# RG-LRU gates of a hybrid encoder layer: two 64-channel blocks on the two row halves of the array

## The chip, the cores and the metric

The kernel runs on one core of one Trainium2 chip. The metric is the device time of one execution in microseconds, the median of several runs. One execution was also taken by the hardware profiler, and all rows shown here come from that one.

## The reference

A layer of 1024 tokens and 1024 channels. The input is normalised and projected, and the columns of the projection are split into query, key, value, the recurrence's input `u`, a GeLU branch `y` and two output gates `g`. Attention and a recurrent branch run on these, are gated and merged, and a feed-forward layer follows. What matters here is the recurrent branch: a depthwise convolution of width 4 over the tokens, and for each of two directions two gates that are block-diagonal products, sixteen blocks of 64 channels.

```python
def block_diag_linear(u, w, b):
    ub = u.reshape(bsz, s, N_REC_BLOCKS, REC_BLOCK)           # 16 blocks of 64
    return jnp.einsum('bsnc,ncd->bsnd', ub, w).reshape(bsz, s, c) + b

def rg_lru(u, w_a, b_a, w_i, b_i, lam, reverse):
    r_gate = sigmoid(block_diag_linear(u, w_a, b_a))
    i_gate = sigmoid(block_diag_linear(u, w_i, b_i))
    log_a = -LRU_C * r_gate * softplus(-lam)
    a = exp(log_a)
    bx = sqrt(max(-expm1(2 * log_a), 0)) * (i_gate * u)
    # h[t] = a[t] * h[t-1] + bx[t], forward or backward over the tokens
```

Both directions' `h` are added, multiplied by `gelu(y)`, and projected.

## The kernel before

**How work is kept.** All tiles have 128 partitions. Activations are held transposed: channels on partitions, 1024 tokens along the free dimension, so the 1024 channels of `u` are eight chunks `j` of 128 channels, and a chunk holds two blocks of 64. Products are made at the accuracy of float32 by splitting each operand into a high and a low part (`split`, line 398: a copy on ScalarE, a subtraction on VectorE) and adding three products: high by high, high by low, low by high. In the profile `wh`, `wl` are the parts of weights, `uh`, `ul` those of a chunk of `u` after the convolution.

**What sets the order.** The kernel doesn't issue instructions as it is written. Every call is recorded as an operation with a position (`SD(pos, fn)`, `M(fn)`), and `solve` (line 210) then runs a list scheduler: each engine takes the available operation with the lowest position, with a cost from a table (`op.cost`, line 179 for TensorE). Buffers are counted too: pool `t` has 45 tiles of SBUF, `w` 9, and PSUM has two banks `pm`, two `pr`, four `pa`. The result is a fixed order per engine; `issue` (line 332) writes it out, all from line 338, which is why every row of the profile names that line. A position is one entry of `main`, which in the projections is six matmuls.

**The stretch of the change.** `pairs` (line 644) makes the projections of `u`, `y`, `g`, `q`, `k` by a scheme with seven products for eight; they use banks `pm` and `pa`. Meanwhile the recurrence runs chunk by chunk (the loop `for j in range(8)`, line 877). Two chunks belong to one entry `("u", i)` of `PORD`; the second begins RSTEP positions after the first (line 848), and its steps stand at fixed positions after its base, divided by RRATE. The steps are:

- `uev`: ScalarE adds the projection's bias to `u`.
- `conv`: one scaled copy on ScalarE, three multiply-adds on VectorE, into `uc`.
- `ucs`: splits `uc` into `uh`, `ul`.
- `gate_pe` (line 909): for each gate (`ty`: 0 recurrence gate, 1 input gate) and direction `d`, six matmuls of 128x128 weights by 128x512 tokens into the two `pr` banks, one bank for each half of the tokens. The weights of a chunk are a 128x128 matrix with its two 64x64 blocks on the diagonal and zeros elsewhere.
- `gate_act` (line 921): a sigmoid on ScalarE from each bank, 512 columns at a time, with a bias per partition; this gives the bank back.
- `iu`, `tanh`, `exp`, `sq`, `m2`, `sqrt`, `scan`: the rest of the recurrence on ScalarE and VectorE; then both directions are added, multiplied by the loaded `y`, and stored as `recd`.

The weights of two chunks come by one load of 512 KB and two splits into pool `w` (`wgj`, line 880). After the projections come attention (from about 500 us, in between with the product of the recurrence's output, `tprod`, line 855) and the rest. `rec_split` (line 1133) splits the reloaded `recd` into `rh`, `rl` for that product. In attention, `a_av` (line 1086) multiplies probabilities `ab` by values `V`: two heads of 64 columns, written to the lower and upper half of the partitions of one bank. DMAs are all issued from SP, in order.

Of the kernel before, what the change touches and what calls it, by code (L numbers as in the profile page):

```python
# [24 lines left out]
for _name, _w in (("g1", 8), ("g2", 8), ("bq", 4), ("bk", 4), ("bu", 8), ("by", 8),  # L25
                  ("bga", 8), ("bgr", 8), ("cw", 32), ("cb", 8), ("ba", 16), ("bi", 16), ("lam", 16)):
    PC[_name] = _n
    _n += _w
# [78 lines left out]
class Plan:  # L107
# [11 lines left out]
    def add(self, eng, meth, args, kw):  # L119
# [57 lines left out]
        if eng == "pe":  # L177
            f32 = isinstance(args[1], VA) and args[1].base.dt == F32
            op.cost = n * 0.84 + 2.6 if meth == "transpose" else (12 if wr[0].box[0][0] else n * 1.68 + 40) if f32 else n * 0.417 + 13.3
# [170 lines left out]
def emit(tc, x, prm, wst, wv, wg, watt, wrec, wout, wff1, wff2, tb, bv, lnf, out):  # L350
# [6 lines left out]
    with ExitStack() as ctx:  # L357
# [490 lines left out]
        RSTEP, RRATE, AOFF, ASTEP = 33.0, 1.0, -6.0, 0.75  # L848
# [25 lines left out]
        wgj = [None] * 4  # L874
        SD(end_of["u", 0] - 12, softplus)

        for j in range(8):
            base = end_of["u", j // 2] + 0.3 + (j % 2) * RSTEP
            if j % 2 == 0:
                wgj[j // 2] = wjob(wg[j // 2], (P, 2, 4, P), base + 2, (22.0, 6.3, 6.0))  # L880
# [5 lines left out]
            def uev(R=R, j=j):  # L886
                R.u = us[j]
                act.activation(R.u, R.u, AF.Identity, bias=col("bu", j), scale=1.0)

            def conv(R=R, j=j):  # L890
                R.uc = T("uc")
                u = R.u
                act.activation(R.uc, u, AF.Identity, bias=col("cb", j), scale=col("cw", 16 + j))
# [7 lines left out]

            def ucs(R=R):
                R.hi = T("uh", F32R)
                R.lo = T("ul", F32R)
                split(R.hi, R.lo, R.uc)
# [3 lines left out]
            def gate_pe(ty, d, R=R, j=j):  # L909
                w = wgj[j // 2]  # L910
                wh = w.hi[:, j % 2, ty * 2 + d, :]
                wl = w.lo[:, j % 2, ty * 2 + d, :]
                pss = R.g[ty, d] = [PR(), PR()]
                for b in range(2):
                    pe.matmul(pss[b], wh, R.hi[:, b * 512:(b + 1) * 512], start=True, stop=False)
                for b in range(2):
                    pe.matmul(pss[b], wh, R.lo[:, b * 512:(b + 1) * 512], start=False, stop=False)
                for b in range(2):
                    pe.matmul(pss[b], wl, R.hi[:, b * 512:(b + 1) * 512], start=False, stop=True)

            def gate_act(ty, d, R=R, j=j):
                pss = R.g[ty, d]
                g = R.g[ty, d] = T("g")
                for b in range(2):
                    act.activation(g[:, b * 512:(b + 1) * 512], pss[b], AF.Sigmoid,
                                   bias=col("ba" if ty == 0 else "bi", d * 8 + j), scale=1.0)
# [40 lines left out]
            SD(base, uev, 30.0)  # L967
            at(1.0, conv)
            at(5.0, ucs)
            for gi, (ty, d) in enumerate(((0, 0), (1, 0), (0, 1), (1, 1))):  # L970
                at(7.5 + 2.5 * gi, lambda ty=ty, d=d, f=gate_pe: f(ty, d))
                at(9.3 + 2.5 * gi, lambda ty=ty, d=d, f=gate_act: f(ty, d))
# [584 lines left out]

def pack(inp):
# [3 lines left out]
    def vec(v):  # L1562
        return np.asarray(v).reshape(-1, P).T

    b_in = inp["b_in"][0]
    cols = [vec(inp["ln1_g"][0]), vec(inp["ln2_g"][0]), vec(b_in[0:512]), vec(b_in[512:1024]),
            vec(b_in[1536:2560]), vec(b_in[2560:3584]), vec(b_in[3584:4608]), vec(b_in[4608:5632]),
            vec(inp["conv_w"][0]), vec(inp["conv_b"][0]), vec(inp["b_rg_a"][0]), vec(inp["b_rg_i"][0]),
# [9 lines left out]
    wg = np.zeros((4, P, 2, 4, P), np.float32)  # L1578
    for ty, nme in enumerate(("w_rg_a", "w_rg_i")):
        w = inp[nme][0]  # L1580
        for d in range(2):
            for j in range(8):
                for b in range(2):
                    wg[j // 2, b * 64:(b + 1) * 64, j % 2, ty * 2 + d, b * 64:(b + 1) * 64] = w[d, 2 * j + b]
# [44 lines left out]
```

## Time and profile before

| | us |
|---|---|
| median of 3 runs | 1419.1 (1418.35 to 1420.6) |
| profiled execution | 1419.8 |
| its span, first to last instruction | 1418.0 |
| TensorE busy | 1402.9 (99%) |
| VectorE busy | 1041.9 (73%) |
| ScalarE busy | 852.0 (60%) |
| mean busy share of the DMA engines | 46% |

A matmul's record begins where it starts and ends when its last column has come out, so records of successive matmuls overlap: the spacing of starts tells what one costs, and a busy TensorE may hold pauses. Weight loads (PEld) are rows of their own, one ahead of each matmul. A row of a timeline can stand for several like instructions; its duration then runs from the first start to the last end.

### The profile page before, as it was taken

The page shows a single profiled execution, that of the slowest core. Times are in us where ns is not written, and L with a number is a line of the kernel's source. Part 1 is how long each engine was busy: PE and PEld are TensorE (multiplying, and loading weights), DVE is VectorE, ACT ScalarE, POOL GpSimd, SP SyncE. Part 2 cuts the span into 40 slices and gives each one's busy share as a digit, 9 for nine tenths or more (in the row PEclk, how much of TensorE's full clock was granted, in tenths as well). Part 3 has the DMA queues.
Part 4 walks back from the last instruction along what each step waited for, and adds up shares of the span by engine and source line. Part 5 has one row for each costly group of instructions (what it writes and reads, how often), then busy time and mean ns, then how long its engine had stood idle before and what let it go on. Part 6 is the DMA issues. An engine that isn't in the chain of part 4 may idle for free.

```text
span 1418.0 us, 17748 instructions
## 1 busy us (share of the span) xinstructions
PE 1402.9 (99%) x6568; PEld 1153.0 (81%) x6568; DVE 1041.9 (73%) x1595; ACT 852.0 (60%) x1316; POOL 0.7 (0%) x6
## 2 busy tenths in 40 slices
PE   8999999999999999999999999999999999999997
PEld 6878888888888887878888888888888888888886
DVE  6897788796985987763945777666666867848996
ACT  7758686877678776764535645654455634423544
POOL 0000000000000000000000000000000000000000
PEclk9999999999999999999999999999999999999999
DMA  6523224233233965747812236444448882245402
GB/s 218 161 62 134 104 97 155 75 134 137 86 104 119 345 225 202 255 146 265 328 61 103 100 116 223 175 156 145 163 163 295 310 327 98 76 173 183 149 15 104
DMA packets 87223, 230.09 MB, mean 162 GB/s; under 512 B 8544, under 2 KB 16864, under 8 KB 87136
## 3 DMA queue, kind: packets, MB, share of 16 engines
q1 hardware_dynamic: 87136, 228.96, 46.2%
q8 instruction: 51, 0.84, 0.2%
q14 instruction: 36, 0.29, 0.1%
HBM read 159.72 MB, written 69.21 MB: 161 GB/s over the span
## 4 chain that ended last, share of the span: by engine, by line
PE 98%; DVE 1%; ACT 0%; DMA 0%; issue 0%
PE pa L338 57%; PE pm L338 28%; PE pr L338 13%; DMA x<-in_x_dram 0%; DVE T4l L338 0%; DVE T1l L338 0%; ACT F L338 0%; DVE F L338 0%; ACT hTh L338 0%; ACT h L338 0%; DVE wl L338 0%; DVE sl L338 0%; DVE hTl L338 0%; DVE T3l L338 0%; DVE nu L338 0%
## 5 line engine op out<-in xcount | busy, mean ns | idle before, releaser
L338 PE MATMUL pa<-wh,rh 128*128 128x512 f32 x448 | 174.0, 389 | 0.0
L338 PE MATMUL pa<-wh,rl 128*128 128x512 f32 x448 | 174.0, 389 | 0.0
L338 PE MATMUL pa<-wl,rh 128*128 128x512 f32 x448 | 173.9, 389 | 0.0
L338 ACT ACTIVATE r<-r 128x1024 f32<-128x1024 f32 x64 | 67.5, 1059 | 67.9 <-DVE r L338 66.9
L338 DVE TENSOR_TENSOR sl<-ws,sh 128x1024 fp32r<-128x1024 f32 x72 | 87.0, 1219 | 19.1 <-ACT sh L338 18.9
L338 ACT ACTIVATE rh<-rs 128x1024 fp32r<-128x1024 f32 x56 | 58.6, 1049 | 67.6 <-PE pa L338 53.5
L338 DVE TENSOR_TENSOR wl<-ws,wh 128x1024 fp32r<-128x1024 f32 x64 | 77.6, 1218 | 29.1 <-ACT wh L338 27.9
L338 PEld LDWEIGHTS pa<-wl,rh 128*128 128x128 f32 x448 | 84.1, 188 | 17.6
L338 PEld LDWEIGHTS pa<-wh,rh 128*128 128x128 f32 x448 | 84.1, 188 | 17.5
L338 PEld LDWEIGHTS pa<-wh,rl 128*128 128x128 f32 x448 | 84.1, 188 | 17.3
L338 ACT ACTIVATE wh<-w 128x1024 fp32r<-128x1024 f32 x56 | 58.8, 1051 | 60.3 <-PE pa L338 44.1
L338 ACT ACTIVATE sh<-ws 128x1024 fp32r<-128x1024 f32 x72 | 75.3, 1054 | 28.0 <-DVE ws L338 27.3
L338 DVE TENSOR_TENSOR acc<-pa,acc 128x512 f32<-128x512 f32 x72 | 49.3, 687 | 51.2 <-PE pa L338 51.1
L338 DVE TENSOR_TENSOR r<-pa,r 128x512 f32<-128x512 f32 x74 | 50.9, 687 | 44.9 <-PE pa L338 44.3
L338 ACT ACTIVATE r<-pm 128x512 f32<-128x512 f32 x81 | 48.0, 592 | 52.5 <-PE pm L338 51.8
L338 ACT ACTIVATE wh<-ws 128x1024 fp32r<-128x1024 f32 x64 | 67.2, 1055 | 15.6 <-DMA ws<-in_watt_dram 8.4
L338 DVE TENSOR_TENSOR wl<-w,wh 128x1024 fp32r<-128x1024 f32 x56 | 68.1, 1218 | 9.3 <-ACT wh L338 5.9
L338 DVE TENSOR_TENSOR rl<-rs,rh 128x1024 fp32r<-128x1024 f32 x56 | 68.1, 1218 | 5.2 <-ACT rh L338 2.9
L338 PE MATMUL pm<-T4h,wx 128*128 128x512 f32 x216 | 71.4, 389 | 0.0
L338 PE MATMUL pa<-T1l,sh 128*128 128x512 f32 x144 | 56.2, 390 | 1.3 <-DVE T1l L338 1.3
L338 PE MATMUL pa<-T1h,sh 128*128 128x512 f32 x144 | 56.1, 389 | 0.0
L338 PE MATMUL pa<-T1h,sl 128*128 128x512 f32 x144 | 56.0, 389 | 0.0
(267 smaller groups left out, 3736.0 us busy)
## 6 DMA issues: line engine op xcount, KB each, us to landing
rs<-rd SPq DMA_DIRECT2D x56, 512.0 KB, 6.7
ws<-in_wst_dram SPq DMA_DIRECT2D x41, 512.0 KB, 4.1
ws<-in_wff_dram SPq DMA_DIRECT2D x38, 512.0 KB, 4.4
w<-in_wff_dram SPq DMA_DIRECT2D x32, 512.0 KB, 7.6
B<-in_tb_dram SPq DMA_DIRECT2D x32, 384.0 KB, 4.6
x<-in_x_dram SPq DMA_DIRECT2D x16, 512.0 KB, 7.8
gd<-r SPq DMA_DIRECT2D x16, 512.0 KB, 2.9
g<-gd SPq DMA_DIRECT2D x16, 512.0 KB, 7.1
```

The lines of the kernel that those rows point to most:

```text
L338: getattr(eng[op.eng], op.meth)(*[r(a) for a in op.args], **{k: r(a) for k, a in op.kw.items()})
```

## The change

The two blocks of a chunk are no longer two corners of one 128x128 matrix. Block 0's input channels lie on partitions 0 to 63, block 1's on 64 to 127, and each gets its own 64x128 weights: 64 columns for the recurrence gate and 64 for the input gate. A matmul then takes 64 partitions of `uh` or `ul`, and is built for a tile of 64 rows and 128 columns, at row 0 for block 0 and at row 64 for block 1. `gate_pe(d, b)` now runs over directions and halves of the tokens, and makes both gates of both blocks: three products for each block, written block 0, block 1, block 0, block 1 and so on, each block into a `pr` bank of its own. The number of matmuls (192) and their columns (512) stay.

Block 0's bank has the recurrence gate on the lower partitions and the input gate on the upper, block 1's the other way round. So after the sigmoids (as many as before, with their own bias columns) `gate_mv` makes three transfers of 64 partitions within SBUF for each direction: the two halves of the input gate into a new tile `gi`, and the missing half of the recurrence gate into block 0's tile, over the half that the first transfer has read.

Besides: the projection's bias of `u` goes into the convolution's constants (`conv_bias`), so `uev` goes, and two small subtractions per chunk mend the first two tokens and the last one, where the convolution sees padding. The weights of four chunks fit one load; they and their parts now live in pool `t`. The planner gets a cost for 64-row matmuls (263 ns of 512 columns for block 0, 12 ns for block 1), and RSTEP and RRATE are changed.

```diff
-            op.cost = n * 0.84 + 2.6 if meth == "transpose" else (12 if wr[0].box[0][0] else n * 1.68 + 40) if f32 else n * 0.417 + 13.3
+            rows = args[1].box[0] if isinstance(args[1], VA) else (0, P)
+            op.cost = (n * 0.417 + 50 if rows[0] == 0 else 12) if rows[1] - rows[0] == 64 else n * 0.84 + 2.6 if meth == "transpose" else (12 if wr[0].box[0][0] else n * 1.68 + 40) if f32 else n * 0.417 + 13.3
...
-        RSTEP, RRATE, AOFF, ASTEP = 33.0, 1.0, -6.0, 0.75
+        RSTEP, RRATE, AOFF, ASTEP = 28.0, 0.9, -6.0, 0.75
...
+        cvb, cve = C("cvb", [P, 8]), C("cve", [P, 8, 3])
+
+        def conv_bias():
+
+            t = C("cvt", [P, 4, 8])
+            for jj in range(4):
+                c = PC["cw"] + jj * 8
+                dve.tensor_mul(t[:, jj], pr[:, c:c + 8], pr[:, PC["bu"]:PC["bu"] + 8])
+            dve.tensor_add(cve[:, :, 0], t[:, 0], t[:, 1])
+            dve.tensor_copy(cve[:, :, 1], t[:, 0])
+            dve.tensor_copy(cve[:, :, 2], t[:, 3])
+            dve.tensor_add(cvb, t[:, 2], t[:, 3])
+            dve.tensor_add(cvb, cvb, cve[:, :, 0])
+            dve.tensor_add(cvb, cvb, pr[:, PC["cb"]:PC["cb"] + 8])
+
+        SD(end_of["u", 0] - 12, conv_bias)
...
-            if j % 2 == 0:
-                wgj[j // 2] = wjob(wg[j // 2], (P, 2, 4, P), base + 2, (22.0, 6.3, 6.0))
+            if j % 4 == 0:
+                wgj[j // 4] = wjob(wg[j // 4], (P, 4, 2, P), base + 2, (22.0, 6.3, 6.0), tag="t", stag="t")
...
-            def uev(R=R, j=j):
-                R.u = us[j]
-                act.activation(R.u, R.u, AF.Identity, bias=col("bu", j), scale=1.0)
+            def conv0(R=R, j=j):
+                R.uc = T("uc")
+                act.activation(R.uc, us[j], AF.Identity, bias=cvb[:, j:j + 1], scale=col("cw", 16 + j))
...
+                dve.tensor_sub(R.uc[:, 0:2], R.uc[:, 0:2], cve[:, j, 0:2])
+                dve.tensor_sub(R.uc[:, S - 1:S], R.uc[:, S - 1:S], cve[:, j, 2:3])
...
-            def gate_pe(ty, d, R=R, j=j):
-                w = wgj[j // 2]
-                wh = w.hi[:, j % 2, ty * 2 + d, :]
-                wl = w.lo[:, j % 2, ty * 2 + d, :]
-                pss = R.g[ty, d] = [PR(), PR()]
-                for b in range(2):
-                    pe.matmul(pss[b], wh, R.hi[:, b * 512:(b + 1) * 512], start=True, stop=False)
-                for b in range(2):
-                    pe.matmul(pss[b], wh, R.lo[:, b * 512:(b + 1) * 512], start=False, stop=False)
-                for b in range(2):
-                    pe.matmul(pss[b], wl, R.hi[:, b * 512:(b + 1) * 512], start=False, stop=True)
-
-            def gate_act(ty, d, R=R, j=j):
-                pss = R.g[ty, d]
-                g = R.g[ty, d] = T("g")
-                for b in range(2):
-                    act.activation(g[:, b * 512:(b + 1) * 512], pss[b], AF.Sigmoid,
-                                   bias=col("ba" if ty == 0 else "bi", d * 8 + j), scale=1.0)
+            def gate_pe(d, b, R=R, j=j):
+
+                w, c = wgj[j // 4], slice(b * 512, (b + 1) * 512)
+                pss = R.g["ps", d, b] = [PR(), PR()]
+                for wt, x in ((w.hi, R.hi), (w.hi, R.lo), (w.lo, R.hi)):
+                    for bl in range(2):
+                        r = slice(bl * 64, (bl + 1) * 64)
+                        pe.matmul(pss[bl], wt[r, j % 4, d, :], x[r, c], start=(wt is w.hi and x is R.hi),
+                                  stop=(wt is w.lo))
+
+            def gate_act(d, b, R=R, j=j):
+                for bl in range(2):
+                    if b == 0:
+                        R.g[bl, d] = T("g")
+                    act.activation(R.g[bl, d][:, b * 512:(b + 1) * 512], R.g["ps", d, b][bl],
+                                   AF.Sigmoid, bias=col("bg2", (d * 8 + j) * 2 + bl), scale=1.0)
+
+            def gate_mv(d, R=R):
+
+                g0, g1, gi = R.g[0, d], R.g[1, d], T("gi")
+                lo, hi = slice(0, 64), slice(64, P)
+                sp.dma_start(gi[lo], g0[hi])
+                sp.dma_start(gi[hi], g1[lo])
+                sp.dma_start(g0[hi], g1[hi])
+                R.g[1, d] = gi
...
-            SD(base, uev, 30.0)
+            SD(base, conv0, 30.0)
             at(1.0, conv)
             at(5.0, ucs)
-            for gi, (ty, d) in enumerate(((0, 0), (1, 0), (0, 1), (1, 1))):
-                at(7.5 + 2.5 * gi, lambda ty=ty, d=d, f=gate_pe: f(ty, d))
-                at(9.3 + 2.5 * gi, lambda ty=ty, d=d, f=gate_act: f(ty, d))
+            for gi, (d, b) in enumerate(((0, 0), (0, 1), (1, 0), (1, 1))):
+                at(7.5 + 2.5 * gi, lambda d=d, b=b, f=gate_pe: f(d, b))
+                at(9.3 + 2.5 * gi, lambda d=d, b=b, f=gate_act: f(d, b))
+                if b:
+                    at(9.4 + 2.5 * gi, lambda d=d, f=gate_mv: f(d))
...
-    wg = np.zeros((4, P, 2, 4, P), np.float32)
+
+    wg = np.empty((2, P, 4, 2, P), np.float32)
     for ty, nme in enumerate(("w_rg_a", "w_rg_i")):
         w = inp[nme][0]
         for d in range(2):
             for j in range(8):
                 for b in range(2):
-                    wg[j // 2, b * 64:(b + 1) * 64, j % 2, ty * 2 + d, b * 64:(b + 1) * 64] = w[d, 2 * j + b]
+                    wg[j // 4, b * 64:(b + 1) * 64, j % 4, d, (ty ^ b) * 64:((ty ^ b) + 1) * 64] = w[d, 2 * j + b]
```

TensorE's order in chunk 1 before: the second half of the input gate, forward, then the recurrence gate, backward. Names are out<-in; `pr_266`, `pr_270` and `pr_271` are banks of the gates, `pa_267` a product of the projections:

```order
L338 MATMUL pr_266_1630<-uh_255_1323,wh_182_1008 128x512
L338 MATMUL pr_266_1630<-ul_256_1485,wh_182_1008 128x512
L338 MATMUL pr_266_1630<-uh_255_1323,wl_183_1065 128x512
L338 MATMUL pa_267_1592<-T1h_158_908,sh_252_1526 128x512
L338 MATMUL pa_267_1592<-T1l_160_1023,sh_252_1526 128x512
L338 MATMUL pa_267_1592<-T1h_158_908,sl_253_1535 128x512
L338 MATMUL pr_270_1640<-uh_255_1323,wh_182_1008 128x512
L338 MATMUL pr_271_1645<-uh_255_1323,wh_182_1008 128x512
L338 MATMUL pr_270_1640<-ul_256_1485,wh_182_1008 128x512
L338 MATMUL pr_271_1645<-ul_256_1485,wh_182_1008 128x512
L338 MATMUL pr_270_1640<-uh_255_1323,wl_183_1065 128x512
L338 MATMUL pr_271_1645<-uh_255_1323,wl_183_1065 128x512
```

The same place after. `pr_267` is block 0's bank (rows 0 to 63), `pr_268` block 1's (rows 64 to 127), and likewise `pr_271` and `pr_272`:

```order
L339 MATMUL pr_267_1623<-uh_249_1523,wh_185_993 128x512
L339 MATMUL pr_267_1623<-ul_250_1579,wh_185_993 128x512
L339 MATMUL pr_267_1623<-uh_249_1523,wl_186_1078 128x512
L339 MATMUL pm_261_1514<-T2h_146_728,sh_251_1541 128x512
L339 MATMUL pm_261_1514<-T2l_148_892,sh_251_1541 128x512
L339 MATMUL pr_268_1634<-uh_249_1523,wh_185_993 128x512
L339 MATMUL pr_268_1634<-ul_250_1579,wh_185_993 128x512
L339 MATMUL pr_268_1634<-uh_249_1523,wl_186_1078 128x512
L339 MATMUL pm_261_1514<-T2h_146_728,sl_252_1556 128x512
```

Block 0's three matmuls stand together, two whole-array matmuls of the projection come between, and then block 1's three: written alternately, they are issued block by block. Further on the order has `pr_271` three times and `pr_272` three times right behind it.

SP's queue about chunk 4, before (`ws` are weight loads, `gd` and `recd` stores):

```order
L338 DMA recd_517_3242<-g_478_2935 128x1024
L338 DMA ws_539_3307<-in_wst_dram 128x1024
L338 DMA gd_544_3319<-r0_522_3197 128x1024
L338 DMA gd_543_3337<-r1_530_3252 128x1024
L338 DMA ws_549_3366<-in_wst_dram 128x1024
```

And after, with the six transfers of a chunk:

```order
L339 DMA gi_430_2635<-g_418_2593 64x1024
L339 DMA gi_430_2635<-g_419_2615 64x1024
L339 DMA recd_420_2667<-gi_375_2334 128x1024
L339 DMA g_418_2593<-g_419_2615 64x1024
L339 DMA gi_443_2686<-g_437_2656 64x1024
L339 DMA gi_443_2686<-g_438_2665 64x1024
L339 DMA g_437_2656<-g_438_2665 64x1024
L339 DMA ws_452_2760<-in_wst_dram 128x1024
```

The transfers stand ahead of a weight load, and the third of each set (`g_418<-g_419`, `g_437<-g_438`) writes what the first reads. SP's queue has 517 rows in place of 471.

## Rows read from the trace of the kernel before

**Rows 1.** The page: TensorE's busy time, and the chain that ended last, by engine.

```profile
PE 1402.9 (99%) x6568; PEld 1153.0 (81%) x6568; DVE 1041.9 (73%) x1595; ACT 852.0 (60%) x1316; POOL 0.7 (0%) x6
...
PE 98%; DVE 1%; ACT 0%; DMA 0%; issue 0%
```

**Rows 2.** Busy time by stretch, seven from 100 to 520 us; first and sum.

```profile
100.00:160.00 60.00, 60.00 (x266) 49.71 (x265) 45.79 (x53) 44.81 (x52) 0.00 (x0) 1.00 0.35 123
...
sum 420.00, PE 420.00 PEld 346.02 DVE 335.38 ACT 322.50 POOL 0.00; mean PE 60.00 PEld 49.43 DVE 47.91 ACT 46.07 POOL 0.00
```

**Rows 3.** Waits from 100 to 460 us: total, times, longest; TensorE's only row.

```profile
PEld pr L338 <- ACT g L338: 1.6, 6, 0.3
```

**Rows 4.** Timeline of TensorE, chunk 0's first gate: start, duration, instruction.

```profile
107.23 0.39 PE L338 MATMUL pm<-hTh,wh 128*128 128x512 f32 x1
...
107.91 0.62 PE L338 MATMUL pr<-uh,wh 128*128 128x512 f32 x2
108.36 0.39 PE L338 MATMUL pm<-hTh,wh 128*128 128x512 f32 x1
108.59 0.39 PE L338 MATMUL pm<-hTl,wh 128*128 128x512 f32 x1
```

**Rows 5.** Groups of TensorE: count, busy us, mean ns; one of three.

```profile
L338 PE MATMUL pr<-uh,wh 128*128 128x512 f32 x64 | 23.4, 398 | 0.0
```

**Rows 6.** Timeline of TensorE about a group of V products.

```profile
644.71 0.40 PE L338 MATMUL pr<-rh,wh 128*128 128x512 f32 x1
645.04 0.88 PE L338 MATMUL pa<-ab,V 128*64 128x128 f32 x12
645.84 0.50 PE L338 MATMUL pm<-rl,wh 128*128 128x512 f32 x1
646.18 0.40 PE L338 MATMUL pr<-rl,wh 128*128 128x512 f32 x1
```

**Rows 7.** Timeline of the weight loads about such a group, idle time before in brackets.

```profile
574.81 0.64 PEld L338 LDWEIGHTS pa<-ab,V 128*64 128x64 f32 x12 [0.35 <-issue]
575.61 0.19 PEld L338 LDWEIGHTS pr<-rl,wh 128*128 128x128 f32 x1 [0.17 <-issue]
```

**Rows 8.** Timeline of TensorE, a whole-array product and three transposes.

```profile
563.55 0.40 PE L338 MATMUL pr<-rh,wl 128*128 128x512 f32 x1
563.78 0.49 PE L338 MATMUL pa<-ident,ab 128*128 128x128 f32 x3
```

**Rows 9.** Groups of weight loads: 128 columns wide, and 64.

```profile
L338 PEld LDWEIGHTS pm<-rh,wh 128*128 128x128 f32 x64 | 12.0, 188 | 1.8
...
L338 PEld LDWEIGHTS pa<-ab,V 128*64 128x64 f32 x384 | 22.2, 136 | 11.0 <-issue 10.6 <-ACT ab L338 0.4
```

**Rows 10.** Groups of ScalarE and VectorE from 90 to 470 us.

```profile
L338 ACT ACTIVATE r<-r,pr 128x1024 f32<-128x1024 f32 x18 | 20.6, 1147 | 4.2 <-DVE r L338 4.2
L338 ACT ACTIVATE wh<-ws 128x1024 fp32r<-128x1024 f32 x21 | 22.1, 1052 | 0.4 <-PE pr L338 0.4
L338 DVE TENSOR_TENSOR sp<-sp,sp 128x16 f32<-128x16 f32 x9 | 1.5, 170 | 0.1
```

**Rows 11.** Transfers of 256 KB, us to landing; waits of SP and for weights.

```profile
V<-vd SPq DMA_DIRECT2D x16, 256.0 KB, 6.9
rd<-r SPq DMA_DIRECT2D x16, 256.0 KB, 2.2
SPq L338 <- PE pm L338: 66.2, 8, 16.8
ACT wx L338 <- DMA ws<-in_wst_dram: 0.7, 1, 0.7
```

**Rows 12.** Timelines: the last split of the recurrence's output, and TensorE's next product.

```profile
525.14 1.23 DVE L338 TENSOR_TENSOR rl<-rec,rh 128x1024 fp32r<-128x1024 f32 x1
527.34 0.40 PE L338 MATMUL pm<-rl,wh 128*128 128x512 f32 x1
```

More of the change, by code (lines that the diff above doesn't have):

```diff
@@ L25 @@
 for _name, _w in (("g1", 8), ("g2", 8), ("bq", 4), ("bk", 4), ("bu", 8), ("by", 8),
-                  ("bga", 8), ("bgr", 8), ("cw", 32), ("cb", 8), ("ba", 16), ("bi", 16), ("lam", 16)):
+                  ("bga", 8), ("bgr", 8), ("cw", 32), ("cb", 8), ("bg2", 32), ("lam", 16)):
     PC[_name] = _n
@@ L873, in emit @@
         rec, recd = [None] * 8, [None] * 8
[L874 removed]
+        wgj = [None] * 2
         SD(end_of["u", 0] - 12, softplus)
+        cvb, cve = C("cvb", [P, 8]), C("cve", [P, 8, 3])
[11 more added lines that the diff above has]
+        SD(end_of["u", 0] - 12, conv_bias)
         for j in range(8):
             base = end_of["u", j // 2] + 0.3 + (j % 2) * RSTEP
[L879 to L880 removed]
+            if j % 4 == 0:
+                wgj[j // 4] = wjob(wg[j // 4], (P, 4, 2, P), base + 2, (22.0, 6.3, 6.0), tag="t", stag="t")
             R = Obj()
@@ L884, in at @@
                 SD(base + us_ / RRATE, fn)
-            def uev(R=R, j=j):
-                R.u = us[j]
-                act.activation(R.u, R.u, AF.Identity, bias=col("bu", j), scale=1.0)
+            def conv0(R=R, j=j):
+                R.uc = T("uc")
+                act.activation(R.uc, us[j], AF.Identity, bias=cvb[:, j:j + 1], scale=col("cw", 16 + j))
             def conv(R=R, j=j):
-                R.uc = T("uc")
-                u = R.u
-                act.activation(R.uc, u, AF.Identity, bias=col("cb", j), scale=col("cw", 16 + j))
+                u = us[j]
                 for jj, sh in ((0, -2), (1, -1), (3, 1)):
@@ L1555, in emit @@
         plan.issue(nc, make)
+SHAPES = {"wg": (2, P, 4, 2, P)}
 def pack(inp):
@@ L1565, in pack @@
     b_in = inp["b_in"][0]
+    bab = np.stack([inp["b_rg_a"][0], inp["b_rg_i"][0]]).reshape(2, 2, 8, 2, 64)
+    bg2 = np.empty((2, 64, 2, 8, 2), np.float32)
+    for b in range(2):
+        for half in range(2):
+            bg2[half, :, :, :, b] = bab[half ^ b, :, :, b].transpose(2, 0, 1)
+    bg2 = bg2.reshape(P, 32)
     cols = [vec(inp["ln1_g"][0]), vec(inp["ln2_g"][0]), vec(b_in[0:512]), vec(b_in[512:1024]),
             vec(b_in[1536:2560]), vec(b_in[2560:3584]), vec(b_in[3584:4608]), vec(b_in[4608:5632]),
-            vec(inp["conv_w"][0]), vec(inp["conv_b"][0]), vec(inp["b_rg_a"][0]), vec(inp["b_rg_i"][0]),
+            vec(inp["conv_w"][0]), vec(inp["conv_b"][0]), bg2,
             vec(inp["lru_lambda"][0])]
```

## The prediction

> **What bounds the kernel now.** I read the page's busy line and the chain of waits first, then the stretch in which the changed code runs, then the matmuls one by one. TensorE is busy for 99% of the span and holds 98% of the chain that ended last [rows 1]. The recurrence runs from about 100 to 460 us, and over the windows from 100 to 520 us TensorE has no idle time at all, while VectorE and ScalarE are busy for 335 and 322 of 420 us [rows 2]. The list of waits of that stretch has one row of the array, a weight load that waits 1.6 us in all for ScalarE [rows 3]. So the clock of this program is the sum of what TensorE's instructions take. A matmul of 128x512 has a record of 0.39 us, but records overlap: from 107.23 to 108.59 us six of them start, (108.59 - 107.23) / 6 = 0.227 us each [rows 4]. I call that a slot. Anything taken from another engine in this stretch is worth nothing by itself; a slot taken from TensorE is worth 0.227 us, and so is an added one.
>
> **What the gates cost before.** Three groups of 64 matmuls, of which one stands in [rows 5], make 192. They are whole-array products whose weights are half zeros, and each takes a slot (two gate matmuls and the next product, 107.91 to 108.36: 0.45 us for two [rows 4]). 192 x 0.227 = 43.6 us.
>
> **Part 1, side by side: what the order leaves of it.** There are still 192 matmuls of 512 columns, but each works on 64 rows, block 0 on the upper half of the array and block 1 on the lower. Two that stand next to each other on different halves can share a slot; two on the same half can't. If all were paired, 96 slots would go. They are not. There are two "pr" banks, each is given back by its own sigmoid, and the planner issues whatever has a bank, so block 0's three matmuls often stand alone, with other products before block 1's three. Counted through TensorE's order, the 192 stand in 50 runs between other work: 20 of three on one half (60 slots), 10 of three on one and then three on the other, where only the third and fourth overlap (5 slots each, 50), 8 of one pair (8), 8 of two pairs (16), 3 of two, two and a pair (4 each, 12), 1 of three pairs (3). That is 149 slots: 43 saved, 43 x 0.227 = 9.8 us.
>
> **Part 2, going into and out of the divided array.** The trace of before has no matmul on 64 rows. It has a divided array of another kind: attention's V products, 64 columns wide on two column halves. From the last whole-array matmul at 644.71 to the second after the group at 646.18 are 1.47 us [rows 6]. Two of the 512-column slots in it are 0.45, so the group of twelve took 1.02. Its own streaming is six pairs of 128 columns. Three transposes of 128 columns fill 0.49 with 275 ns for one record, so their starts are (0.49 - 0.275) / 2 = 0.108 apart [rows 8], and six are 0.65: that the twelve need no more shows that the two halves do run side by side. By the twelve's own record, (0.88 - 0.273) / 5 = 0.121, it is 0.73 at most [rows 6]. So 0.29 to 0.37 us of each group is neither. Where it lies is plain in the weight loads: ordinarily a load runs under the matmul before it, but the first of the group waits 0.35 and the first after it 0.17, for nothing that the profile shows [rows 7]. It isn't the data type or the transposes: from a 512-column matmul to a transpose on the whole array is 563.55 to 563.78, an ordinary slot [rows 8]. So entering and leaving the divided array each costs a pause in which the old products run out and the new weights come in.
>
> The gates' loads are 128 columns wide, not 64: 188 against 136 ns [rows 9], 0.05 more at the entry. For a run of gates I take 0.40 us (0.36 + 0.05, rounded), with 0.29 and 0.42 as the bounds if the row halves behave as the column halves do, and 0 as the bound if they change without a pause. I take 0.40 because attention's group is the only divided array in the trace and pays in every case I looked at. 50 x 0.40 = 20.0 us.
>
> The page "TensorEngine Tiling (Array Packing)" of the Trainium skill (section Tiling Modes, Key Properties) says that a change of tiling mode, as against a change of tile, drains the engine. The V rows agree for column halves, with 0.29 to 0.37 us; that it holds for row halves no run here shows. By it the sum is the one below; without it, the first rival.
>
> **Part 3, attention's groups.** They too are re-planned: whole to 64 columns and back 42 times in before's order, 39 in after's. 3 x 0.36 = 1.1 us gained.
>
> **Part 4, what lies beside TensorE.** The bias of u goes into the convolution's constants: eight ScalarE passes of 1.147 us fall away (9.2 us), and sixteen VectorE corrections of one or two columns come, at the 0.17 us of the smallest operations (2.7 us) [rows 10]. Two gate-weight loads of four, with two splits on ScalarE (1.05 each [rows 10]) and two on VectorE, go. The sigmoids keep count and size. All at nothing, covered by a TensorE that waits for nobody there; without the cover ScalarE would be 11 us shorter. 48 transfers of 256 KB come. The nearest rows land in 2.2 us (a store) to 6.9 us (a gather) [rows 11]. The third of each set overwrites what the first reads, so it waits on SP until the first has landed, and weight loads queue behind it: 16 such holds, 35 us of SP at 2.2. SP already waits 66 us on one kind of product alone in this stretch, and yet ScalarE waited only 0.7 us for weights [rows 11], so I take nothing. Between sigmoid and use there are now two transfers in a row, 4.4 to 13.8 us. The chunks overlap, so this reaches TensorE only after the last one. RSTEP, RRATE move the second chunk of each pair 5 positions forward and stretch its steps by 1/0.9; a position is six slots, 1.36 us.
>
> **Sum.** -9.8 (shared slots) + 20.0 (pauses) - 1.1 = **+9.1 us**. The profiled execution took 1419.8 (span 1418.0), so 1428.9; the median of the runs is 0.7 lower, 1428.2. I put down 1428.5. With 0.29 it is +3.6, about 1423; with 0.42 and a microsecond or two of new waits 1432 to 1433.
>
> **Rivals.**
> - *Row halves change without a pause.* Then 43 slots and three groups are gained: -9.8 - 1.1 = -10.9, about 1408.5. For it: the two halves of rows hold separate weights, and no row of before shows how they change over. Against: the column halves of the same array pause both ways. 0.23.
> - *Only one way pauses*, 0.2 a run: 10.0 - 10.9 = -0.9, about 1418. This is also where gain and loss meet: at (9.8 + 1.1) / 50 = 0.22 us a run the change is worth nothing. 0.08.
> - *It doesn't do what it says*: the two halves stream one after the other, 192 slots as before, and the pauses come on top: 20.0 - 1.1 = +18.9, about 1438. Against it: the V groups overlap. For it: those move 128 columns of another type. 0.07.
> - *The transfers come late.* In before, the last split of the recurrence's output ends at 526.37 and TensorE takes up a product of its kind at 527.34: 1.0 us to spare [rows 12]. The last chunk starts 5 positions earlier, but its last step stands at 35 positions in place of 31.5, so it is 1.5 positions (2.0 us) early, plus the spare. Two transfers of 2.2 leave 1.4 us of waiting, two of 6.9 leave 10.8, on top of the forecast: 1430 to 1439. It decides from 3.0 us on for the two. The plan knows a transfer's length and can place other products first. 0.04 for more than 3 us.
>
> **How the numbers follow.** The forecast (pause both ways, halves overlap) has 0.58, with a range of its own of 1423 to 1433. About 0.2% (2.8 us) is what runs of this kernel can tell from no change. Faster: the first rival and the low end of the second, 0.25. Same: the rest of the second and the lowest corner of the forecast, 0.08. Slower: 0.67. The range has to reach the first rival, since leaving it out along with the two slow ones would leave out a third: 1408 to 1433 leaves out the lower half of that rival and the two slow ones, some 0.2.
>
> **What would show it.** In after, the gate matmuls should stand in runs; inside a run of pairs two starts should lie within some 10 ns, then 0.227 to the next two; the first weight load of each run and the first after it should sit idle for "issue" by 0.2 to 0.35 us. If those idle times are missing and the matmul after a run starts one slot behind it, the first rival is right. If starts inside a pair are 0.227 apart, the halves don't overlap. If TensorE's waits show rl or wh between 440 and 540 us, the transfers are late. What would make all of it wrong is idle time of TensorE elsewhere that grew because the new plan moved other work.

## The result, and the profile after

The changed kernel takes 1430.4 us (median of four runs, 1429.8 to 1430.9) against 1418.9 for the kernel before: ratio 1.0079, 95% interval 1.0061 to 1.0096, so 11.5 us slower. The prediction was 1428.5, with 67% on slower. Its profiled execution took 1430.7 (span 1429.0) against 1419.8 (1418.0): +11.0 us, and this is the difference that is accounted for below.

The page of the kernel after, its busy line and its chain by engine (compare [rows 1]):

```profile
PE 1410.0 (99%) x6568; PEld 1133.8 (79%) x6568; DVE 1041.6 (73%) x1619; ACT 840.6 (59%) x1306; POOL 0.7 (0%) x6
...
PE 96%; DVE 2%; ACT 1%; issue 0%; DMA 0%; DVEq 0%
```

TensorE still does as many instructions, is still busy for 99%, and its busy time grew by 7.1 us. The chain now has 3% of VectorE and ScalarE. ScalarE got lighter by 11 us, as it was to, and that brought nothing.

**The pauses.** Timeline of TensorE in the kernel after (start, duration, instruction), a run of three gate matmuls on one half between whole-array products:

```profile
121.20 0.39 PE L339 MATMUL pm<-T3h,sl 128*128 128x512 f32 x1
121.52 0.50 PE L339 MATMUL pr<-uh,wh 64*128 64x512 f32 x1
121.86 0.39 PE L339 MATMUL pr<-ul,wh 64*128 64x512 f32 x1
122.09 0.39 PE L339 MATMUL pr<-uh,wl 64*128 64x512 f32 x1
122.41 0.50 PE L339 MATMUL pm<-T3h,sh 128*128 128x512 f32 x1
122.74 0.40 PE L339 MATMUL pm<-T3l,sh 128*128 128x512 f32 x1
```

Read the starts, not the durations. Inside the run they are 0.23 apart. Across the entry two steps take 0.32 + 0.34 in place of 2 x 0.227, and across the exit 0.32 + 0.33 again: about 0.2 us more each. From the last whole product to the second after the run are 1.54 us; its five slots are 1.13; the pause of this run is 0.41. It appears nowhere as idle time: a record covers the start of the next, so the page counts TensorE as busy throughout. (The profile models the ends of TensorE's records, it doesn't see them; so only starts are compared here.)

The same view, and the weight loads under it, for a run of six, in which the program's order has block 0's three ahead of block 1's three:

```profile
162.96 0.40 PE L339 MATMUL pm<-T2l,sh 128*128 128x512 f32 x1
163.28 0.51 PE L339 MATMUL pr<-uh,wh 64*128 64x512 f32 x2
163.62 0.40 PE L339 MATMUL pr<-ul,wh 64*128 64x512 f32 x2
163.85 0.40 PE L339 MATMUL pr<-uh,wl 64*128 64x512 f32 x2
164.18 0.51 PE L339 MATMUL pm<-T2h,sl 128*128 128x512 f32 x1
```

```profile
163.28 0.19 PEld L339 LDWEIGHTS pr<-uh,wh 64*128 64x128 f32 x2 [0.36 <-issue]
...
164.18 0.19 PEld L339 LDWEIGHTS pm<-T2h,sl 128*128 128x128 f32 x1 [0.36 <-issue]
```

Each line "x2" holds one matmul of either half, and two together take no longer than one alone: 0.40. They ran as three pairs (uh,wh of both blocks, ul,wh of both, uh,wl of both) although the program issued them as three and three. And the first load of the run and the first behind it are idle for 0.36 each with nothing to wait for: the sign that the prediction asked for (compare [rows 7]).

Seven of the ten runs in this order are three pairs. In the other three, block 1's half began 0.07, 0.32 and 0.38 us after block 0's and stayed behind. Each time it began 0.05 to 0.06 us after the end of the sigmoid that gave its bank back, as here on ScalarE (two sigmoids, to 405.34) and TensorE:

```profile
404.07 1.27 ACT L339 ACTIVATE g<-pr,pr 128x512 f32<-128x512 f32 x2
```

```profile
405.01 0.49 PE L339 MATMUL pr<-uh,wh 64*128 64x512 f32 x1
405.34 0.39 PE L339 MATMUL pr<-ul,wh 64*128 64x512 f32 x1
405.39 0.49 PE L339 MATMUL pr<-uh,wh 64*128 64x512 f32 x1
```

Groups of the gate matmuls over the whole span, count, busy us, mean ns (before: [rows 5], 23.4 us for one such group of three):

```profile
L339 PE MATMUL pr<-uh,wh 64*128 64x512 f32 x64 | 22.1, 505 | 0.3 <-ACT g L339 0.3
...
L339 PE MATMUL pr<-ul,wh 64*128 64x512 f32 x64 | 18.5, 425 | 0.0
L339 PE MATMUL pr<-uh,wl 64*128 64x512 f32 x64 | 17.8, 401 | 0.0
```

uh,wh stands first in most runs, so its mean record, 505 ns, carries the entry.

**A stall that was not forecast.** Busy time by stretch in the kernel after; columns are the stretch, its length, busy us (count) of TensorE, its weight loads, VectorE, ScalarE and GpSimd, then the granted clock, the DMA share and GB/s:

```profile
100.00:290.00 190.00, 190.00 (x821) 143.88 (x821) 145.47 (x167) 135.53 (x160) 0.00 (x0) 1.00 0.41 133
290.00:302.00 12.00, 10.44 (x32) 5.84 (x30) 11.93 (x12) 8.13 (x12) 0.00 (x0) 0.72 0.58 191
...
294.80:301.60 6.80, 6.46 (x18) 3.88 (x17) 6.76 (x8) 3.82 (x7) 0.00 (x0) 0.50 0.71 223
```

And before:

```profile
283.00:295.00 12.00, 12.00 (x55) 9.94 (x54) 11.95 (x10) 9.60 (x15) 0.00 (x0) 1.00 0.28 95
```

Before, such a stretch held 55 matmuls in its 12 us; here it holds 32, and the granted clock is 0.72 in the mean. What stands in it on ScalarE, TensorE and VectorE, by time:

```profile
290.50 0.69 ACT L339 ACTIVATE g<-pr,pr 128x512 f32<-128x512 f32 x1 [5.11 <-PE pr L339]
291.08 1.99 ACT L339 ACTIVATE sh<-ws 128x1024 fp32r<-128x1024 f32 x2
```

```profile
293.12 0.50 PE L339 MATMUL pa<-T1h,sh 128*128 128x512 f32 x1 [0.89 <-ACT sh L339]
...
295.66 0.79 PE L339 MATMUL pa<-T1h,sl 128*128 128x512 f32 x1 [0.34 <-DVE sl L339]
296.25 0.63 PE L339 MATMUL pa<-T1h,sh 128*128 128x512 f32 x1
296.67 0.63 PE L339 MATMUL pa<-T1l,sh 128*128 128x512 f32 x1
```

```profile
287.47 1.22 DVE L339 TENSOR_TENSOR ul<-uc,uh 128x1024 fp32r<-128x1024 f32 x1
...
293.27 2.33 DVE L339 TENSOR_TENSOR sl<-ws,sh 128x1024 fp32r<-128x1024 f32 x2
```

ScalarE takes its work in the program's order. A gate's sigmoid stands 5.1 us at its head, because its last matmuls come only at 289.73: they use `ul`, which VectorE finishes at 288.69. The weight split sh stands behind it, VectorE's sl behind that, and TensorE runs out of split weights: it waits 0.9 us for sh, 0.3 for a gate's bank, and at 295.66 0.3 for sl. After the first two waits the clock falls: from 294.8 to 301.6 us it is 0.50 (last row of the stretches), the 1.2 GHz level, and two products start 0.42 apart (296.25 to 296.67) in place of 0.227. It lasts 6.8 us, of which half, 3.4, is lost. With the waits, 1.6 in all, that is about 5 us. No wait for a transfer stands in this chain; the nearest is one of 0.9 us on VectorE at 264.7.

**The account of +11.0 us**, worked out from the starts and ends of TensorE's records in both traces:

| term | predicted | measured |
|---|---|---|
| gate matmuls, streaming alone | -9.8 | 44.3 to 30.6: -13.7 |
| 50 runs, in and out | +20.0 (0.40 each) | 100 changes of about 0.205: +20 |
| attention's groups, 42 to 39 | -1.1 | -1.0 to -1.6 |
| anything beside TensorE | 0 | stall near 290 us: about +5 |
| sum | +9.1 | +10 to +11 |

The changed kernel is also 0.7 us ahead when the recurrence begins (counted through, the same matmul starts at 95.5 us in place of 96.1). What is left, some 1 us, is spread over the first matmuls behind each run, whose starts are up to 0.235 apart rather than 0.227.

### The profile page after: what moved, and what is told of

It reads as the page before. It is cut to its first block, busy times and chain, and to the rows that moved or that the text cites. A ratio compares the mean times of both kernels' runs of the same rounds, so it can differ in the third digit from the quotient of the medians.

```text
span 1429.0 us, 17867 instructions
## 1 busy us (share of the span) xinstructions
PE 1410.0 (99%) x6568; PEld 1133.8 (79%) x6568; DVE 1041.6 (73%) x1619; ACT 840.6 (59%) x1306; POOL 0.7 (0%) x6
## 4 chain that ended last, share of the span: by engine, by line
PE 96%; DVE 2%; ACT 1%; issue 0%; DMA 0%; DVEq 0%
PE pa L339 55%; PE pm L339 27%; PE pr L339 13%; DVE gi L339 0%; DMA x<-in_x_dram 0%; ACT h L339 0%; ACT L339 0%; DVE T4l L339 0%; DVE ws L339 0%; DVE sl L339 0%; DVE T1l L339 0%; DVE h L339 0%; ACT hTh L339 0%; ACT wh L339 0%; DVE r L339 0%
## 5 line engine op out<-in xcount | busy, mean ns | idle before, releaser
L339 ACT ACTIVATE g<-pr,pr 128x512 f32<-128x512 f32 x64 | 42.2, 686 | 34.2 <-PE pr L339 29.0
```

Of the source, the lines that this page charges most:

```text
L339: getattr(eng[op.eng], op.meth)(*[r(a) for a in op.args], **{k: r(a) for k, a in op.kw.items()})
```

## The experiments

The theory after the result: the array pauses by 0.41 us for each run of gate matmuls, and the stall is a matter of what the change adds beside TensorE. The rivals: the loss is in the fold, the spacing or the transfers and not in the array; the halves are served in order; the stall comes of the planner's costs, of the two banks, or of SP's queue. Each experiment starts from the changed kernel (line 339), unless it says otherwise; "held" kernels (line 351) have a function more. Ratios are against the kernel before, run beside it.

**1. Everything but the divided array.** The gate matmuls cover the whole array again, with zeros in half of the weights; the fold, the order of the halves, the transfers and the spacing stay. The gate weights, twice as large so, come by four loads again.

```diff
-                        r = slice(bl * 64, (bl + 1) * 64)
-                        pe.matmul(pss[bl], wt[r, j % 4, d, :], x[r, c], ...
+                        pe.matmul(pss[bl], wt[:, j % 2, d, bl, :], x[:, c], ...
...
-SHAPES = {"wg": (2, P, 4, 2, P)}
+SHAPES = {"wg": (4, P, 2, 2, 2, P)}
```

> The changed kernel with everything kept (bias fold, transfers, spacing), but each gate matmul on the whole array, with zeros in the weights for the other block's 64 rows; gate weights back in pool w, two chunks per load. 192 slots as before, no run of a divided array, 39 groups of attention's V products. Theory of the pauses (each of the 50 runs costs 0.41 us to enter and leave, and the plan that thinks gates too cheap makes the stall about 290 us): nothing of either is left, 1417 to 1419 us. Rival, the transfers and the new plan are what costs: the loss stays in part, 1424 us or more.

Measured: 1419.0, ratio 0.9999 (0.9990 to 1.0009). TensorE waits 0.5 us in the recurrence's stretch. So the fold, the transfers and the spacing cost nothing that shows by themselves, and the 11 us, the stall too, come only with the divided array (and the two weight loads that it saves).

**2. Three pairs in every run.** The six matmuls of a gate are held together: the first waits for both banks and all operands, and the five others follow at once. 32 runs in place of 50.

```diff
+                        if first is None:
+                            first = op
+                            for o in ready:
+                                op.preds[o.idx] = 1
+                            plan.hold(op, pss)
+                            plan.boost += 1000.0
...
+                plan.boost -= 1000.0
```

> The changed kernel with the six matmuls of a gate kept in one run: the first waits for both banks and for all four operands, the other five follow at once. 32 runs of three pairs in place of 50 runs. Pauses: 96 slots x 0.227 = 21.8 and 32 x 0.41 = 13.1 against 43.5 before, and four groups of V fewer (-1.4): 10 us faster than before, 1409 us, up to 1416 if a stall like the one about 290 us comes again. Rival, the transfers and the plan cost 6 us or more by themselves: 1415 us or more, without one place that stalls. Rival, the gates wait so long for two banks that TensorE idles: slower than the changed kernel, over 1430 us.

Measured: 1424.3, ratio 1.0039 (1.0024 to 1.0054): 8 to 15 us over what I expected. The runs are as meant and the pauses too, but TensorE's waits from 100 to 475 us (total, times, longest) are new:

```profile
PE pa L351 <- ACT sh L351: 4.0, 4, 1.8
PE pa L351 <- DVE sl L351: 1.6, 3, 0.6
```

They are the same splits as in the stall of the changed kernel, at 199, 221, 269 and 288 us, again with a stretch of half clock behind them (6.8 us from 292). So the gain of fewer runs went into stalls. The next runs ask what makes these.

**3. A cost in the plan.** The planner counts a pair of half-array matmuls at 276 ns, 264 of them on the one that works on the lower rows and 12 on the other. Here each counts 266 by itself, so the plan's clock for TensorE runs slower and nearer to what a run with its pauses takes.

```diff
-            op.cost = (n * 0.417 + 50 if rows[0] == 0 else 12) if rows[1] - rows[0] == 64 ...
+            op.cost = (n * 0.417 + 53) if rows[1] - rows[0] == 64 ...
```

> The changed kernel, but the planner's cost of every 64-row matmul is 266 ns (what they took on average in the changed kernel, pauses included) in place of 263 for block 0 and 12 for block 1. 47 runs, 117 slots by the order. If the stall about 290 us comes of a plan that has TensorE ahead of what it does: gone, and 26.5 + 47 x 0.41 - 1.1 - 43.5 = +1.2, 1420 us. If the stall comes of transfers or buffers: it stays, 1426 to 1430 us.

Measured: 1425.1, ratio 1.0043 (1.0028 to 1.0058). The stall is gone, as expected: TensorE has no wait in the recurrence. 5.3 us came back, from 1430.4, of which some 2 are three runs fewer (1.2) and less streaming (0.7). The total is 5 over the forecast: the gate matmuls take 29.9 us where I had counted 26.5. Twelve runs of six have matmuls of one half ahead of the other's, and in seven of them the other half began 0.1 to 0.6 us late (2.7 us more in all from first to last start), each time 0.05 to 0.06 us after the sigmoid that gave its bank back.

**4. The changed kernel without the transfers.** The 48 transfers that sort the halves are left out, so the gates of two channel blocks stay in each other's places.

```diff
-                sp.dma_start(gi[lo], g0[hi])
-                sp.dma_start(gi[hi], g1[lo])
-                sp.dma_start(g0[hi], g1[hi])
-                R.g[1, d] = gi
+                pass
```

> The changed kernel without the 48 transfers: the sorting of the gates' halves is left out, so the recurrence takes mixed gates. 47 runs, 125 slots by the order, 36 groups of V. If transfers and SP's queue cost the part that pauses don't explain (6 to 7 us): 28.3 + 19.3 - 2.2 - 43.5 = +1.9, 1421 us. If that part comes of the plan's cost for TensorE: a stall of several us stays somewhere between 100 and 460 us, 1425 to 1430 us.

Measured: 1421.8, ratio 1.0019 (1.0010 to 1.0029), and no wait of TensorE in the recurrence. Without the transfers there is no stall. But leaving them out also gives the planner less to place, and its order is another one (47 runs in place of 50), so this doesn't show by itself that the transfers hold anything up.

**5. The true price in the plan of the held runs.** As 2, but the planner knows what a run takes: three slots and a pause.

```diff
+                        op.cost = 0.1
...
+                            op.cost = 3 * 226.7 + 405.0
```

> Runs of six as in e2_run6, and the planner is told what a run takes: 3 x 227 + 405 ns, all on its first matmul. Theory: the stalls of e2_run6 (TensorE waits for sh and sl, then 6.8 us at half clock) come of a plan in which TensorE is ahead of itself; with the true cost they go and 21.8 + 32 x 0.42 - 43.5 - 5 x 0.36 = -10 is left: 1409 to 1411 us. Rival, the stalls come of holding both banks and of the transfers: they stay, 1420 to 1425 us.

Measured: 1419.1, ratio 1.0000 (0.9991 to 1.0009). Five better than 2, and still 8 to 10 over what I expected. TensorE still waits 4.5 us, mostly for one split or another, and its clock is 0.50 for 3.4 us from 273 us:

```profile
PE pm L351 <- ACT wh L351: 1.6, 1, 1.6
PE pa L351 <- ACT sh L351: 1.4, 1, 1.4
```

Ahead of one of these ScalarE itself waits for a sorted gate (start, duration, instruction, idle time ahead of it):

```profile
217.96 1.16 ACT L351 ACTIVATE th<-g,spp 128x1024 f32<-128x1024 f32 x1 [1.68 <-DMA g<-g]
...
221.48 1.04 ACT L351 ACTIVATE sh<-ws 128x1024 fp32r<-128x1024 f32 x1
```

The transfer holds th, and the split sh at 221.48 is later in the same order.

**6. Held runs without the transfers.** As 5, with the sorting left out as in 4.

> e2t_run6cost without the 48 transfers: the sorting of the gates' halves is left out, so the recurrence takes mixed gates. e2t_run6cost lost some 7 us to waits of TensorE for splits of weights near 221 and 269 us (with 3.4 us at half clock), although the plan had the true cost. If the transfers, which ScalarE's tanh and VectorE's products wait for in order, make these splits late: the waits go, 1409 to 1412 us. If the planner's order of ScalarE and VectorE does it without them: 1416 to 1420 us.

Measured: 1409.5, ratio 0.9930 (0.9914 to 0.9947). TensorE waits for nothing from 100 to 475 us, while ScalarE waits for gate matmuls about as long as in the changed kernel (total, times, longest; there 29.0, 22, 5.1):

```profile
ACT g L351 <- PE pr L351: 33.2, 23, 5.2
```

This is the account of the pauses without anything else in it: 32 runs of three slots are 21.8 us of streaming, 22 less than before, and 32 x 0.41 = 13.1 of pauses; -8.7 together, -10.5 with five V groups fewer, and -10.9 was measured. It says two things of the stalls: they go with the transfers (9.6 us between 5 and 6, of which 4.5 were waits of TensorE and 1.7 were lost at half clock; the planner's order changes here too), and a sigmoid that stands 5 us at ScalarE's head costs TensorE nothing when what is queued behind it is not yet due.

**7. In which order the halves are served.** As 5, but a run is written as block 0's three and then block 1's three.

```diff
-                for wt, x in ((w.hi, R.hi), (w.hi, R.lo), (w.lo, R.hi)):
-                    for bl in range(2):
+                for bl in range(2):
+                    for wt, x in ((w.hi, R.hi), (w.hi, R.lo), (w.lo, R.hi)):
```

> e2t_run6cost with the six matmuls of a run issued block by block: three on the upper rows, then three on the lower. If matmuls start in the order of issue, only the third and the fourth overlap, 5 slots in place of 3: 32 x 2 x 0.227 = 14.5 us more than e2t_run6cost. If a half takes its next matmul without waiting for the other half's that stand ahead: the same time as e2t_run6cost, and starts in pairs some 10 ns apart.

Measured: 1419.0, ratio 0.9997 (0.9987 to 1.0006), equal to 5. In 31 of the 32 runs the starts are in pairs; in one the second half came 0.40 us late, again 0.05 after the sigmoid that gave its bank back. A half that could not pass the other's queued matmuls would have cost two slots more in each of 32 runs, 14.5 us. The timeline of TensorE has pairs:

```profile
159.72 0.39 PE L351 MATMUL pm<-hTh,wl 128*128 128x512 f32 x1
160.04 0.50 PE L351 MATMUL pr<-uh,wh 64*128 64x512 f32 x2
160.38 0.40 PE L351 MATMUL pr<-ul,wh 64*128 64x512 f32 x2
160.61 0.40 PE L351 MATMUL pr<-uh,wl 64*128 64x512 f32 x2
160.94 0.50 PE L351 MATMUL pm<-hTh,wh 128*128 128x512 f32 x1
```

**8. Twelve in a run.** The two token halves of a direction are computed in one held run, the second six into banks of the other pool, with the run's true price in the plan. 16 runs.

```diff
-                pss = R.g["ps", d, b] = [PR(), PR()]
+                R.g["ps", d, 0], R.g["ps", d, 1] = [PR(), PR()], [PA(), PA()]
...
+                                op.cost = 6 * 226.7 + 405.0
```

> Twelve matmuls of a direction (both halves of the tokens) in one run, the second six into two banks of pool pa; the planner is told 6 x 227 + 405 ns. 16 runs. Pauses: 21.8 + 16 x 0.42 - 43.5 - 4 x 0.36 = -16.4, 1402 to 1404 us. Rival, four banks held at once make the projections' products wait: several us of waits of TensorE between 100 and 460 us, 1408 us or more.

Measured: 1408.6, ratio 0.9926 (0.9911 to 0.9941): 10.5 us faster than the kernel before and 22 faster than the change, with all of the sorting in it. A run of twelve in its timeline:

```profile
194.70 0.39 PE L351 MATMUL pm<-hTh,wl 128*128 128x512 f32 x1
195.02 0.50 PE L351 MATMUL pr<-uh,wh 64*128 64x512 f32 x2
195.35 0.40 PE L351 MATMUL pr<-ul,wh 64*128 64x512 f32 x2
195.59 0.40 PE L351 MATMUL pr<-uh,wl 64*128 64x512 f32 x2
195.82 0.40 PE L351 MATMUL pa<-uh,wh 64*128 64x512 f32 x2
196.06 0.39 PE L351 MATMUL pa<-ul,wh 64*128 64x512 f32 x2
196.28 0.40 PE L351 MATMUL pa<-uh,wl 64*128 64x512 f32 x2
196.61 0.50 PE L351 MATMUL pm<-hTh,wh 128*128 128x512 f32 x1
196.94 0.40 PE L351 MATMUL pm<-hTl,wh 128*128 128x512 f32 x1
```

194.70 to 196.94 are 2.24 us: eight slots, 1.81, and a pause of 0.43 for twelve matmuls as for three. It fell 5 to 7 us short of what I expected. Waits of TensorE are left, 2.7 us in all (1.6 for ScalarE's r, 0.7 for wh, 0.4 for a bank), and in four of the 16 runs the starts aren't in pairs.

**9. Twelve in a run with the changed kernel's costs.** As 8 without the two lines on the price.

> e3t_run12 with the planner's cost for 64-row matmuls as in the changed kernel (263 and 12 ns, so 1.65 us for a run of twelve that takes 1.77). If a true cost in the plan is what keeps the stalls away: some stall of several us comes, 1412 us or more. If the number of runs is what matters and the plan's cost hardly does: within 2 us of e3t_run12, 1407 to 1411 us.

Measured: 1413.9, ratio 0.9959 (0.9944 to 0.9974). The price in the plan is worth 5.3 us here, as it was worth 5.2 between 2 and 5.

**10. The spacing of before.** The changed kernel with the old spacing of the chunks.

```diff
-        RSTEP, RRATE, AOFF, ASTEP = 28.0, 0.9, -6.0, 0.75
+        RSTEP, RRATE, AOFF, ASTEP = 33.0, 1.0, -6.0, 0.75
```

> The changed kernel with RSTEP and RRATE as before (33 and 1.0). 49 runs. If the stall about 290 us hangs on how closely the chunks follow each other: gone, about 1424 us. If it hangs on the plan's cost for TensorE or on the transfers whatever the spacing: a stall of several us stays, 1428 us or more.

Measured: 1435.2, ratio 1.0113 (1.0098 to 1.0128), 4.8 slower than the change. The stall moves and grows; TensorE waits 7.1 us in four places, the longest:

```profile
PE pm L339 <- ACT sh L339: 3.6, 1, 3.6
```

So the new spacing doesn't make it, and its numbers are the better ones for the divided array. Between experiment 1, which has them, and the kernel before, no difference shows.

**11 and 12. Is it SP's queue?** Each set's third transfer waits on SP for the first, and weight loads queue behind. Here the transfers are issued from GpSimd, which is otherwise idle (0.7 us busy in the page): 11 is 5 with that, 12 is 8 with it. The planner charges such an issue as it does one from SP.

```diff
-                sp.dma_start(gi[lo], g0[hi])
-                sp.dma_start(gi[hi], g1[lo])
-                sp.dma_start(g0[hi], g1[hi])
+                pool.dma_start(gi[lo], g0[hi])
+                pool.dma_start(gi[hi], g1[lo])
+                pool.dma_start(g0[hi], g1[hi])
```

> e2t_run6cost with the 48 transfers kept, but issued from GpSimd's queue, which is otherwise empty, in place of SP's. If it is SP's order that makes them late (a transfer that waits for a sigmoid or for the landing of the first holds what is queued behind it, and waits behind other stores itself): the waits of TensorE go, 1409 to 1413 us. If it is their own length: they stay, 1416 to 1420 us.

> e3t_run12 with the transfers issued from GpSimd's queue. If SP's order costs there what it costs with runs of six: the few us of waits that e3t_run12 has left shrink, 1403 to 1407 us. If their own length does: 1407 to 1410 us, as e3t_run12.

Measured: 1431.4, ratio 1.0082 (1.0067 to 1.0097), and 1416.0, ratio 0.9977 (0.9967 to 0.9986): 12.4 and 7.4 us worse than from SP. So what else stands in SP's queue is not what makes the transfers late, and the theory that had it so falls. In 11 the wait for the first transfer is now GpSimd's, and the last transfer is late for ScalarE more often than in 5 (there 5.9 us in 3):

```profile
POOL g L351 <- DMA gi<-g: 31.4, 12, 5.9
...
ACT th L351 <- DMA g<-g: 12.8, 7, 4.6
```

The transfers themselves land about as fast as in the changed kernel, where SP issues them: 3.5 and 3.1 us here, 3.1 and 3.3 there. The loss of 11 against 5 stands in TensorE's waits, 11.8 us against 4.5, and in four stretches of 3.4 us at half clock against one (first and last, columns as above):

```profile
180.60:184.00 3.40, 3.40 (x9) 2.65 (x9) 3.36 (x6) 3.12 (x3) 0.00 (x0) 0.50 0.00 0
...
317.20:320.60 3.40, 3.40 (x9) 2.64 (x8) 2.62 (x3) 3.37 (x3) 0.00 (x0) 0.51 0.00 0
```

Half of three such stretches is 5.1 us; with 7.3 of waits that is 12.4. The test isn't a clean one: the transfers still wait for each other in GpSimd's order, and they go by another kind of queue (`software_dynamic` in the page, 3840 packets).

## Why the prediction was right, and where two of its steps were not

- **The pause: right.** 0.40 us a run was taken from attention's column halves; row halves pause by 0.41 to 0.43, whether a run has 3, 6 or 12 matmuls, and the sum over the runs is 20 as predicted. It is shown by the spacing in every kernel, by experiment 1 (no division, no loss), and by 6 and 8, where 18 and 34 runs fewer make the kernel faster than before. The rule of "TensorEngine Tiling (Array Packing)" in the Trainium skill (Tiling Modes, Key Properties), that a change of mode drains the engine, agrees with this trace for row halves too, at 0.41 us for the two changes of a run.
- **What the sharing saves: mis-sized.** "10 of three on one and then three on the other, where only the third and fourth overlap (5 slots each, 50)" is the step that failed. A half doesn't wait for matmuls of the other half that stand ahead: seven of the ten ran as three pairs, 3 slots each, and in experiment 7, which has this order throughout, 31 of 32 did. With all of them so, and the runs of two, two and a pair too, the 149 slots would be 126. The records show 30.6 us, 135 slots' worth: four late halves are 0.9 us of the difference, a run at half clock 0.4, and the rest is in starts behind an entry that are 0.235 apart rather than 0.227. The saving was 13.7, not 9.8.
- **Nothing beside TensorE: wrong by 5 us.** "All at nothing" held for the fold and the spacing (experiment 1), and "I take nothing" of the transfers held only there, with the array whole. The prediction looked for their price at the last chunk, as waits for rl or wh between 440 and 540 us; it came at 290 us, in the middle, where the chunks overlap, as a wait for split weights of another stage. The step that misled was "the chunks overlap, so this reaches TensorE only after the last one": the engines take their work in the program's order, so a late gate in one chunk holds up the splits that TensorE needs for another. In the stall itself the gate was late for `ul`; that the transfers have a part in it is known from experiments 4 and 6 alone. What the prediction named as making all of it wrong, idle time of TensorE elsewhere that grew because the plan moved other work, is what happened, at a size that the other miss covered.
- **The V groups: right,** -1.0 to -1.6 for -1.1.

So the forecast was 2 us low by two misses of 4 and 5 us with opposite signs; that it came so near is luck. It was right about the sign for the reason it gave: 50 runs at 0.41, some 20 us, cost more than the 13.7 of sharing and the V groups save, by some 5 us even without the stall. Sharing in runs of six saves three slots, 0.68, and pays; the 20 runs of three on one half save nothing and pay 0.41 each.

The rivals: no pause, and one pause a run, are out by the timeline; halves that don't overlap are out by the lines "x2". The late transfers, as far as they make the stall, came in another place.

**What stays open.** In these runs stalls come only with both the transfers (4 and 6 have none and don't stall) and the divided array (1 has the transfers and doesn't stall), and are lessened where the plan's price is changed (3) or knows a run's pause (5 against 2, 8 against 9). The new spacing is ruled out as the cause, and so is the other work in SP's queue; that the transfers wait for each other is not. Which property of the transfers does it, their two in a row or the time to landing that the plan assumes, wasn't told apart: no run changed a transfer's length in the plan or sorted the halves with one transfer in place of two. Why experiment 3, whose costs are no truer for every run, has no stall at all was not settled either; that its order happens to leave room is only an argument.

## What to carry to other kernels

A matmul on half of the array shares its time with one on the other half if both have their banks, but a run of them between whole-array work pays a fixed pause of 0.41 us here, against 0.227 saved for a pair of 512 columns: two pairs in a run just pay, one doesn't, and a run on one half alone is pure loss, so make the runs long before dividing anything. Count the runs in the order as it is issued, not the matmuls, and read the pause in the spacing of the starts, since no idle time shows it. And when an operation's price changes, the planner that orders the work around it has to be told: it was worth 5 us twice.

## What the runs showed of the hardware that was not expected

- Two row halves don't keep to a common order: with three matmuls of one half issued ahead of three of the other, both start together, some 10 ns apart, and the run takes three slots (1419.0 us against 1419.1 with the pairs written side by side). Where a half began late, 0.05 to 0.06 us behind the sigmoid that freed its bank, the other half went on without it (eleven runs of the changed kernel and experiment 3).
- The pause comes whether the array is divided by rows (0.41 to 0.43) or by columns (0.29 to 0.37 with narrower weight loads [rows 6]), and for rows it hardly depends on a run's length (3, 6 or 12 matmuls).
- In the changed kernel TensorE waited 0.9 us until 293.1 and 0.3 until 294.2; from 294.8 us the granted clock stood at 0.50, the 1.2 GHz level, for 6.8 us, in which 3.4 were lost: twice what its waits took. In experiments 5, 7, 9, 10 and 12 there was one such stretch of 3.4 us in the recurrence, in 11 there were four.
- The same small transfers issued from an idle GpSimd made the kernel 7 to 12 us slower than from a busy SP, with much the same time from issue to landing. Where the loss stands is shown (waits and clock of TensorE), why it comes is not.
